# A fused attention and convolution step on one core: queries and keys of a head asked for nine blocks ahead, two V buffers, weights asked for twelve steps earlier

## The chip, the cores and the metric

The kernel runs on one core of a Trainium2 chip. The metric is the device time of one execution in microseconds (us); the program before was run three times. Traces and profile come from one execution taken by the hardware profiler.

## What is computed

One layer of a streaming encoder over 1024 prompt frames and 32 sample frames (the 32 next frames of a stream with 512 cached ones), width 1024. Cut to what matters here:

```python
h = rmsnorm(x, norm_g)                       # 1056 frames x 1024
q, k, v, f, ga, ua, ub, gb, ma, mb = split(h @ w_in)
q, k = rmsnorm(q) * 64 ** -0.5, rmsnorm(k)   # 16 heads of 64
c = cumsum(log_sigmoid(f + b_f))             # one forget sum per head
p = softmax(causal(q @ k.T + c_q - c_k))     # per head
ya = (p @ v * silu(ga)) @ w_pa
u = ua * sigmoid(ub)                         # causal depthwise conv, 31 taps
yb = (silu(layernorm(conv(u))) * silu(gb)) @ w_pb
y = x + (sigmoid(ma) * ya + sigmoid(mb) * yb) @ w_out
```

Outputs are y, the keys, values, forget logs and the last 30 convolution rows.

## The kernel before, in words

Channels lie on partitions, the 1056 frames on the free axis. Each projection is done for 128 output channels at a time (`steps`): three chunks of 352 frames, each summed over eight slices of 128 input channels, each slice as three float16 matmuls (high weights by high input, low by high, high by low, L183). One slice is one **step**: three matmuls, then `beat()`, which runs what the planner has put at this step.

**Weights** come in batches of two blocks (`Batch`). A batch is loaded as two `raw` tiles (L109, four buffers), its power is measured (ACT `junk` L117, POOL `topb` L120, PE `tot` L126, DVE `sc` L157), and it is split into `wh` (ACT L138) and `wl` (DVE L141). `begin()` runs when the first block of a batch is projected, and sets the next batch's work at fixed steps from there: measured at 3 and 13, split at 29 and 39, its last `wl` pieces at 34 and 44; and it asks for the raw weights of the batch after that at steps 17 and 27. A batch is 48 steps.

**Stages**, in order: the token rows are turned and the first convolution block projected (`x_split`, in three column chunks, with a table of jobs by step); the values; the convolution inputs with the keys and queries between them, which go to scratch in DRAM (`s_k`, `s_q`, each a high and a low part); the gate `ga`; attention, beside which the gates `gb`, `ma` and `mb` are projected; then three output projections.

**Attention.** `seq` holds 16 heads of eight blocks (`Block`, 128 queries each); four `Sample` blocks for the cached stream are put in after the first block of heads 3, 7, 11 and 15. Loop step n works on `seq[n]`: `start(seq[n + 3])` makes the scores of the block three further on (`QB` by `KB` L1094, `QA` by `KA` L1095); then mask and maximum (DVE L1097, L1099), exponent (ACT L1102), scaling (POOL L1105); `turn()` transposes the probabilities of `seq[n]` (PE `ptr` L1119, copied by ACT or DVE L1122); `fill(4)` does four steps of a gate projection, whose chunk is read out by ACT into one of three `t` tiles (L930, L932) and stored by a DMA (L933). That projection has one PSUM bank (`pq`). Two loop steps after the last block of a head, `values()` multiplies by V (PE `po`, forty matmuls, L1138), ACT and DVE put the result into `ot` (L1142, L1143; in odd heads L1145 multiplies by the gate `ga`, loaded at L1127), and in odd heads a DMA stores it (L1147).

A head's queries and keys are eight DMAs on SP's queue (`Head.load`, L948 to L955: six of 256 KB, two of 16 KB), into two sets of buffers in turn. They are asked for when `seq[n + 5]` is the head's first block, that is in block 3 of the head before; the head's first scores are made in block 5 of it. V is one DMA (L962) into a single buffer, asked for after the values of the head before.

**Orders.** In attention the orders of PE and SP are those of the code; SP takes its DMAs strictly one after another, and one that waits (for data, for a buffer, or for the DMA eight before it to have landed) holds up those behind it. The other engines' orders there come from the scheduler's own simulated time. In the stages before, PE, DVE and ACT stand in the order of the code and SP's is the scheduler's.

Of the kernel before, what the change touches and what calls it, by code (L numbers as in the profile page):

```python
# [8 lines left out]
F32 = mybir.dt.float32  # L9
# [13 lines left out]
H = 16  # L23
# [30 lines left out]
def build(tc, xT, xt, wv, wf, ckT, cv, clT, stT, vec, cst, yT, kT, vO, lfO, cpT, csT):  # L54
# [4 lines left out]
    def pool(name, bufs=1, stack=es, **kw):  # L59
        return stack.enter_context(tc.tile_pool(name=name, bufs=bufs, reuse_waits="tile", **kw))  # L60
# [29 lines left out]
    class Batch:  # L90
# [31 lines left out]
        def total(self):  # L122
            pool, tag = totals[-1]
            self.ps = pool.tile([128, 512], F32, name="tot", tag=tag)
            if self.n == 2:
                nc.tensor.matmul(self.ps[:, :2], ones_b, self.topb, start=True, stop=True)  # L126
            else:
                for i in range(2):
                    nc.tensor.matmul(self.ps[:, 0:1], ones_b, self.topb[:, i:i + 1], start=(i == 0), stop=(i == 1))
# [7 lines left out]
        def high(self, i, wh, raw, ks):  # L137
            nc.scalar.mul(wh[:, ks, :], raw[:, ks, :], self.s[:, i:i + 1])  # L138

        def low(self, i, wl, wh, raw, ks):  # L140
            nc.vector.scalar_tensor_tensor(wl[:, ks, :], raw[:, ks, :], self.s[:, i:i + 1], wh[:, ks, :],  # L141
                                           op0=ALU.mult, op1=ALU.subtract)
# [78 lines left out]
    def begin():  # L221

        if not plan:
            return
        b = plan.pop(0)
        after = plan[0] if plan else None
        t = pace["tick"]
        jobs = [(25, b.total), (27, b.power)]
        if b.n == 2:
            jobs += [(3, lambda: b.stage(0)), (13, lambda: b.stage(1))]  # L230
            for i, n in ((0, 29), (1, 39)):
                jobs.append((n, lambda i=i: b.split(i)))
                jobs += [(n + 1 + 2 * p, lambda i=i, p=p: b.rest(i, p)) for p in range(3)]
        else:
            jobs += [(3 + 10 * i, lambda i=i: b.stage(i)) for i in range(2)]
            jobs.append((29, lambda: split.__setitem__(b.keys[0], split_v(b.keys[0][1], b))))
        if after:
            jobs += [(17 + 10 * i, after.load) for i in range(after.n)]
        prep.extend((t + n, fn) for n, fn in sorted(jobs, key=lambda e: e[0]))

    def steps(key, rh, rl, pspool, evac):
# [38 lines left out]
    class Banks:  # L280

        n = 0
# [230 lines left out]
    def squares(t, act=True, sl=slice(0, D), acc=None):  # L513
        r = rows(t)
        acc = rs9[:r, t:t + 1] if acc is None else acc
        sq = xip.tile([128, D], F32, name="sq", tag="sq", bufs=2)[:r, sl]
        x = xtok[t][:r, sl]
        if act:
            nc.scalar.activation(sq, x, AF.Square, accum_out=acc)
        else:  # L520
            nc.vector.scalar_tensor_tensor(sq, x, 1.0, x, op0=ALU.mult, op1=ALU.mult, accum_out=acc)

    def root(t0, nt):

        rs = rs9[:, t0:t0 + nt]
        v, y = [xip.tile([128, 4], F32, name=f"n4{i}", tag=f"n4{i}", bufs=2)[:, :nt] for i in range(2)]
        nc.vector.tensor_scalar(v, rs, 1.0 / D, EPS, op0=ALU.mult, op1=ALU.add)
        nc.scalar.activation(y, v, AF.Ln)
        nc.scalar.activation(y, y, AF.Exp, scale=-0.5)
        return lambda: newton(rs, v, y)  # L530

    def scale(t, h, pool=False):
        r = rows(t)
        x, f = xtok[t][:r, half[h]], rs9[:r, t:t + 1]
        if pool:
            nc.gpsimd.tensor_scalar(x, x, f, 1.0, op0=ALU.mult, op1=ALU.mult)
        else:
            nc.vector.tensor_scalar(x, x, f, None, op0=ALU.mult)
# [60 lines left out]
    def known(i):  # L599
        recs[i].power(psq[:, i + 1:i + 2], 1)  # L600
# [23 lines left out]
    def rooted(t0, nt):  # L624
        steps_of[t0] = root(t0, nt)
# [12 lines left out]
    for f in range(8):  # L638
# [14 lines left out]
    x_split(0, ws0, u0, {  # L653
        0: [lambda: top(1), lambda: squares(2, False)],
        1: [lambda: squares(3)],
        2: [lambda: total(2), lambda: high(0, 1), lambda: low(0, 1)],
        3: [lambda: known(1), lambda: squares(4, False), lambda: high(1, 0), lambda: low(1, 0)],
        4: [lambda: rooted(2, 3), lambda: high(0, 2)],
        5: [lambda: steps_of[2](), lambda: scale(2, 0), lambda: scale(3, 0, True), lambda: scale(4, 0), lambda: low(0, 2)],
        6: [lambda: scale(3, 1, True), lambda: scale(2, 1), lambda: high(1, 1), lambda: low(1, 1)],  # L660
        7: [lambda: scale(4, 1), lambda: high(1, 2), lambda: low(1, 2)]})
# [38 lines left out]
    def split_v(c, rec):  # L700
        wh2, wl2, raws2 = [], [], rec.raws
        for raw in raws2:
            with tc.high_priority(offset=1500):
                wh, wl = [vp.tile([128, 4, VC], F16, name=a, tag=a, bufs=4) for a in ("vwh", "vwl")]
                rec.high(0, wh, raw, slice(0, 4))
                for k in (0, 2):
                    rec.low(0, wl, wh, raw, slice(k, k + 2))
            wh2.append(wh)
            wl2.append(wl)

        def running():
            ps = pj.tile([128, 512], F32, name="pjs", tag="pj")
            for n in range(2):
                for j in range(4):
                    nc.tensor.matmul(ps[32 * j:32 * j + 32, :VC], xsm[:, 2 * j + n, :],
                                     raws2[j // 2][:, (2 * j + n) % 4, :], start=(n == 0), stop=(n == 1))
            pace["credit"] -= 1.3
            later(4, lambda: gathered(ps))

        def gathered(ps):  # L720
            v4 = vp.tile([TS, 4, VC], F32, name="v4", tag="v4", bufs=1)
            for j in range(4):
                nc.scalar.copy(v4[:, j, :], ps[32 * j:32 * j + 32, :VC])
            vs = vp.tile([TS, VC], F32, name="vs", tag="vs", bufs=1)
            nc.vector.tensor_reduce(vs, v4.rearrange("p j n -> p n j"), axis=AX.X, op=ALU.add)
            nc.vector.tensor_copy(z[:TS, 8, 4 * c:4 * c + 4], vs[:, 256:])
            nc.sync.dma_start(vO[T:, 256 * c:256 * c + 256], vs[:, :256])
            nc.sync.dma_start(s_vs[:, 256 * c:256 * c + 256], vs[:, :256])

        later(14, running)  # L730
        return wh2, wl2, rec.inv
# [4 lines left out]
    for c in range(4):  # L736
# [13 lines left out]
        pace["rate"] = R_V  # L750
        wh2, wl2, inv = split.pop(("v", c))
        begin()
        for t in range(8):
            ps = pj.tile([128, 512], F32, name="pjv", tag="pj")
            n = 0
# [181 lines left out]
    class Head:  # L937
# [20 lines left out]

        def load_v(self):
            h = self.h  # L960
            self.V = hp.tile([128, 8, 64], F32, name="V", tag="V", bufs=1)
            nc.sync.dma_start(self.V, s_v[:, :, 64 * h:64 * h + 64].rearrange("b t d -> t b d"))  # L962

    pace["rate"] = R_U
# [3 lines left out]
    hp = pool("hp", 2, stack=p2, side="right")  # L968
    heads = [Head(h) for h in range(H)]
# [31 lines left out]
    def fill(n):  # L1001
        for _ in range(n):
            next(flow, None)
# [145 lines left out]
    seq = []  # L1149
# [5 lines left out]
    def start(b):  # L1155
        if getattr(b, "i", 1) == 0:
            h = b.head
            if h.h % 2 == 0:
                h.ot = heads[h.h + 1].ot = ap.tile([128, T], F32, name="ot", tag="ot", bufs=2)
        b.scores()  # L1160

    def pending(b):
        return isinstance(b, Sample) or b.i % 2
# [36 lines left out]
    ln = layernorm()  # L1200
    sides["shift"] = ap.tile([128, TT], F32, name="shift", bufs=1)
    nc.sync.dma_start(sides["shift"], s_m)
    start(seq[0])
    fill(8)
    start(seq[1])
# [2 lines left out]
    for n, b in enumerate(seq):  # L1208
        if n + 3 < len(seq):
            start(seq[n + 3])  # L1210
        if n + 5 < len(seq) and getattr(seq[n + 5], "i", 1) == 0:
            seq[n + 5].head.load()
        if n + 6 < len(seq) and isinstance(seq[n + 6], Sample):
            seq[n + 6].load()
        if isinstance(b, Sample):
            fill(4)
            b.turn()
        else:
            b.turn()
            fill(4 if b.i > 2 or b.head.h != 8 else 0)  # L1220
        if n >= 2 and pending(seq[n - 2]):
            seq[n - 2].values()
        if n >= 3 and isinstance(seq[n - 3], Sample):
            seq[n - 3].finish()
        if n >= 2 and getattr(seq[n - 2], "i", 0) == 7 and seq[n - 2].head.h + 1 < H:
            heads[seq[n - 2].head.h + 1].load_v()
        if "ready" in sides:
            next(ln, None)
    for b in seq[-2:]:
# [16 lines left out]
    class Banks3:  # L1246
        n = 0
# [383 lines left out]
```

## Time and profile before

| what | us |
|---|---|
| median of three runs | 1451.53 |
| lowest and highest run | 1445.54, 1453.81 |
| the profiled execution | 1445.9 |
| its span in the trace | 1443.9 |
| stage: start, to the first values | 0 to 60 |
| stage: values and convolution inputs | 60 to 215 |
| stage: keys, queries, convolution inputs, gate ga | 215 to 577 |
| stage: attention with gates | 577 to about 1155 |
| stage: output projections | 1155 to 1444 |

How to read it: a row of the windows view gives for each engine the busy time in that stretch and the number of instructions, then the clock that TensorE was granted (1.00 is full), the share of time that the DMA engines were busy, and the rate. A row of the waits view names who waited, for whom, the total in us, how often, and the longest. A row of the timeline gives start, length, engine, line, operation, tiles, and in brackets the idle time just before it with what ended it. A row of the chain gives start, length and the piece of work on the chain that ended last.

### The profile page before, as it was taken

What the parts mean: (1) busy time and instruction counts of PE and PEld (TensorE: products, weight loads), DVE (VectorE), ACT (ScalarE), POOL (GpSimd) and SP (SyncE); (2) the same over time, 40 slices, a digit from 0 to 9 for tenths busy, and PEclk for the clock granted to TensorE, in tenths of its full rate; (3) what the DMA queues carried; (4) which work ended last, traced back from release to release, by engine and by line L of the source; (5) the groups of instructions that cost most, each with busy time, mean ns of one, the idle gap of its engine ahead of it and who ended that gap; (6) DMA issues with size and microseconds to landing.
All of it is one profiled execution on the core that took longest, in us unless ns stands there. A gap on an engine that the chain in (4) does not pass through costs nothing.

```text
span 1443.9 us, 24762 instructions
## 1 busy us (share of the span) xinstructions
PE 1347.8 (93%) x9383; PEld 1020.0 (71%) x9383; DVE 976.5 (68%) x1534; ACT 723.0 (50%) x1360; POOL 496.5 (34%) x548
## 2 busy tenths in 40 slices
PE   8999999999999999787989788978888999999999
PEld 5687866666666666565666566656665689999999
DVE  6787888869798988656767645544444459455664
ACT  6544547575768535444544454534543465423321
POOL 2000126265748302333333322211211228545653
PEclk9999999999999999999999999999999999999999
DMA  6242434373435232335343543453444197743462
GB/s 233 92 148 85 125 89 130 109 195 116 131 121 168 100 128 95 99 102 148 108 130 107 155 116 83 121 149 88 116 116 124 49 359 258 233 135 120 144 202 73
DMA packets 113495, 194.96 MB, mean 135 GB/s; under 512 B 34080, under 2 KB 80032, under 8 KB 113376
## 3 DMA queue, kind: packets, MB, share of 16 engines
q1 hardware_dynamic: 113232, 193.31, 43.9%
q8 instruction: 74, 1.21, 0.4%
q14 instruction: 45, 0.37, 0.1%
q10 hardware_dynamic: 144, 0.07, 0.0%
HBM read 127.68 MB, written 65.64 MB: 134 GB/s over the span
## 4 chain that ended last, share of the span: by engine, by line
PE 71%; DMA 10%; DVE 5%; SPq 5%; ACT 4%; issue 3%; POOL 1%; ACTq 0%; DVEq 0%; POOLq 0%
PE pj L183 47%; PE pjv L760 6%; PE pj L1463 5%; PE po L1138 5%; DMA KA<-s_ak 5%; PE ptr L1119 3%; DMA raw<-wf 2%; DMA KA<-s_k 2%; PE psS L1095 1%; DVE y L368 1%; PE psS L1094 1%; ACT t L932 1%; DVE nm L1099 1%; DVE wl L141 1%; ACT P L1102 1%
## 5 line engine op out<-in xcount | busy, mean ns | idle before, releaser
L183 PE MATMUL pj<-xh,wh 128*128 128x352 f16 (+2 forms) x1536 | 489.0, 318 | 8.2 <-ACT t L932 6.9
L183 PE MATMUL pj<-xh,wl 128*128 128x352 f16 (+2 forms) x1536 | 488.1, 318 | 0.7 <-DVE wl L141 0.6
L183 PE MATMUL pj<-xl,wh 128*128 128x352 f16 (+2 forms) x1536 | 487.5, 317 | 0.1
L183 PEld LDWEIGHTS <-wh 128*128 128x128 f16 x3072 | 305.4, 99 | 165.4 <-issue 2.6
L368 DVE SCALAR_TENSOR_TENSOR y<-u,vec_t,y 128x1086 f32<-128x1086 f32 x240 | 342.6, 1428 | 9.5 <-ACT y L365 6.6
L1105 POOL TENSOR_SCALAR P<-P,nm 128x128 f32<-128x128 f32 (+7 forms) x128 | 119.1, 931 | 336.7 <-DVE nm L1104 281.7
L183 PEld LDWEIGHTS <-wl 128*128 128x128 f16 x1536 | 152.6, 99 | 84.4 <-issue 10.7
L141 DVE SCALAR_TENSOR_TENSOR wl<-raw,sc,wh 128x384 f16<-128x384 f32 (+1 forms) x192 | 119.1, 655 | 30.5 <-ACT wh L138 30.5
L1122 ACT COPY pt<-ptr 128x512 f32<-128x512 f32 (+3 forms) x128 | 64.4, 503 | 143.9 <-PE ptr L1119 143.3
L1102 ACT ACTIVATE P<-psS,nm 128x128 f32<-128x128 f32 (+7 forms) x128 | 94.8, 741 | 65.5 <-DVE nm L1099 52.0
L1094 PE MATMUL psS<-KB,QB 128*128 128x256 f32 (+2 forms) x192 | 82.7, 432 | 39.7 <-DMA KB<-s_k 33.8
L1097 DVE TENSOR_TENSOR psS<-psS,cmask 128x128 f32<-128x128 f32 x128 | 37.7, 295 | 118.2 <-PE psS L1095 117.7
L1099 DVE TENSOR_REDUCE nm<-psS 128x1 f32<-128x128 f32 (+7 forms) x128 | 96.3, 754 | 8.5 <-DVE psS L1097 0.5
L1095 PE MATMUL psS<-KA,QA 68*128 68x256 f32 (+2 forms) x192 | 70.1, 366 | 30.1 <-DMA KA<-s_ak 24.6
L1119 PE MATMUL ptr<-ident,P 128*128 128x128 f32 x576 | 93.6, 294 | 1.2 <-ACT pt L1122 1.2
L175 POOL TENSOR_TENSOR wl<-raw,wh 128x384 fp32r<-128x384 f32 (+1 forms) x51 | 63.4, 1271 | 74.6 <-ACT wh L172 58.7
L1119 PEld LDWEIGHTS ptr<-ident,P 128*128 128x128 f32 x576 | 77.2, 153 | 6.9 <-ACT pt L1122 1.5
L1094 PEld LDWEIGHTS psS<-KB,QB 128*128 128x128 f32 x192 | 37.5, 195 | 57.3 <-issue 39.9
L138 ACT ACTIVATE wh<-raw,sc 128x1024 f16<-128x1024 f32 (+1 forms) x68 | 72.7, 1089 | 7.8 <-DVE sc L158 7.5
L869 POOL TENSOR_TENSOR sql<-sqf,sqh 128x352 fp32r<-128x352 f32 x48 | 58.7, 1224 | 50.7 <-ACT sqh L866 50.6
L1138 PE MATMUL po<-pt,V 128*64 128x256 f32 x640 | 72.8, 382 | 0.3 <-ACT pts L1051 0.3
L117 ACT ACTIVATE junk<-raw 128x1024 bf16<-128x1024 f32 x62 | 65.2, 1052 | 12.9 <-DMA raw<-wf 12.8
(271 smaller groups left out, 2574.8 us busy)
## 6 DMA issues: line engine op xcount, KB each, us to landing
raw<-wf SPq DMA_DIRECT2D x92, 512.0 KB
QB<-s_q SPq DMA_DIRECT2D x32, 256.0 KB
KB<-s_k SPq DMA_DIRECT2D x32, 256.0 KB
kT<-qn SPq DMA_DIRECT2D x8, 528.0 KB
s_ga<-t SPq DMA_DIRECT2D x24, 176.0 KB
s_gb<-t SPq DMA_DIRECT2D x24, 176.0 KB
s_ma<-t SPq DMA_DIRECT2D x24, 176.0 KB
s_mb<-t SPq DMA_DIRECT2D x24, 176.0 KB
```

The source lines that it names most:

```text
L138: nc.scalar.mul(wh[:, ks, :], raw[:, ks, :], self.s[:, i:i + 1])
L141: nc.vector.scalar_tensor_tensor(wl[:, ks, :], raw[:, ks, :], self.s[:, i:i + 1], wh[:, ks, :], op0=ALU.mult, op1=ALU.subtract)
L183: nc.tensor.matmul(ps, a[:, kt, :], b(kt, sl), start=(first and n == 0), stop=(last and n == N - 1))
L368: t = nc.vector.scalar_tensor_tensor(y, u[:, i:i + CW], w, y, op0=ALU.mult, op1=ALU.add)
L760: nc.tensor.matmul(ps[:, :VC], a, b, start=(n == 0), stop=(n == 23))
L1094: nc.tensor.matmul(ps[:, b, :wm], QB[:, qsl], KB[:, ksl], start=True, stop=False)
L1095: nc.tensor.matmul(ps[:, b, :wm], QA[:, qsl], KA[:, ksl], start=False, stop=True)
L1099: nc.vector.tensor_reduce(nm[:, 0:1], ps[:, :nb, :w], axis=AX.XY, op=ALU.max, negate=True)
L1102: nc.scalar.activation(P[:, :nk].rearrange("p (b w) -> p b w", b=nb), ps[:, :nb, :w], AF.Exp, bias=nm[:, 0:1], accum_out=nm[:, 1:2])
L1105: nc.gpsimd.tensor_scalar(P[:, :nk], P[:, :nk], nm[:, 2:3], 1.0, op0=ALU.mult, op1=ALU.mult)
L1119: nc.tensor.transpose(pt[:, 128 * j:128 * j + 128], P[:, 128 * (4 * u + j):128 * (4 * u + j) + 128], ident)
L1138: nc.tensor.matmul(po[rows], V[:, j, :], parts[c][:, j, :], start=(c % 2 == 0 and j < 2), stop=(c % 2 == 1 and j >= 2 * c))
```

## The change

Five edits: `after.load` stands at steps 5 and 15 instead of 17 and 27; in the first chunk of `x_split` the power of the second weight block (`total(2)`, `known(1)`, `high(1, 0)`, `low(1, 0)`) comes one step later; V has two buffers; a head's queries and keys are asked for nine blocks ahead, those of head 1 before the loop; the next head's V is asked for in block 3.

```diff
@@ Batch planning, begin() @@
-            jobs += [(17 + 10 * i, after.load) for i in range(after.n)]
+            jobs += [(5 + 10 * i, after.load) for i in range(after.n)]
@@ x_split(0, ...) @@
-        2: [lambda: total(2), lambda: high(0, 1), lambda: low(0, 1)],
-        3: [lambda: known(1), lambda: squares(4, False), lambda: high(1, 0), lambda: low(1, 0)],
-        4: [lambda: rooted(2, 3), lambda: high(0, 2)],
+        2: [lambda: high(0, 1), lambda: low(0, 1)],
+        3: [lambda: total(2), lambda: squares(4, False)],
+        4: [lambda: known(1), lambda: rooted(2, 3), lambda: high(1, 0), lambda: low(1, 0), lambda: high(0, 2)],
@@ Head.load_v @@
-            self.V = hp.tile([128, 8, 64], F32, name="V", tag="V", bufs=1)
+            self.V = hp.tile([128, 8, 64], F32, name="V", tag="V", bufs=2)
@@ before the attention loop @@
     nc.sync.dma_start(sides["shift"], s_m)
+    heads[1].load()
     start(seq[0])
@@ the attention loop @@
-        if n + 5 < len(seq) and getattr(seq[n + 5], "i", 1) == 0:
-            seq[n + 5].head.load()
+        if n + 9 < len(seq) and getattr(seq[n + 9], "i", 1) == 0:
+            seq[n + 9].head.load()
         if n + 6 < len(seq) and isinstance(seq[n + 6], Sample):
             seq[n + 6].load()
+        if getattr(b, "i", 0) == 3 and b.head.h + 1 < H:
+            heads[b.head.h + 1].load_v()
...
-        if n >= 2 and getattr(seq[n - 2], "i", 0) == 7 and seq[n - 2].head.h + 1 < H:
-            heads[seq[n - 2].head.h + 1].load_v()
```

First place: SP's queue in attention around head 4, before the change. `s_gb<-t` is a gate store, `s_o<-ot` the attention output of heads 2 and 3, V the values of head 4, and the eight rows after it head 5's queries and keys.

```order
L1127 DMA ga<-s_ga 128x1024
L933 DMA s_gb<-t 128x352
L1147 DMA s_o<-ot 128x1024
L962 DMA V<-s_v 128x8x64
L948 DMA QB<-s_q 64x1024
L949 DMA QB<-s_q 64x1024
L950 DMA KB<-s_k 64x1024
L951 DMA KB<-s_k 64x1024
L952 DMA QA<-s_q 64x1024
L953 DMA QA<-s_aq 4x1024
L954 DMA KA<-s_k 64x1024
L955 DMA KA<-s_ak 4x1024
```

The same place after the change. V is now head 5's, asked for in block 3 of head 4, and the queries and keys at the end, of which the first rows are shown, are head 6's, asked for in block 7 of head 4.

```order
L1127 DMA ga<-s_ga 128x1024
L109 DMA raw<-wf 128x1024
L933 DMA s_gb<-t 128x352
L1147 DMA s_o<-ot 128x1024
L962 DMA V<-s_v 128x8x64
L109 DMA raw<-wf 128x1024
L933 DMA s_gb<-t 128x352 x2
L948 DMA QB<-s_q 64x1024
L949 DMA QB<-s_q 64x1024
L950 DMA KB<-s_k 64x1024
L951 DMA KB<-s_k 64x1024
```

The eight loads no longer stand right behind the output store and the V load: they come six blocks ahead of the head's first scores instead of two, and V is asked for six blocks ahead of its use.

Second place: SP's queue in the stage of keys and queries, where the scheduler had put head 0's load among the stores of a query block (`s_q<-qh`, `s_q<-ql`). Rows with a minus leave this place.

```order
-L109 DMA raw<-wf 128x1024
-L896 DMA s_q<-ql 128x352
-L109 DMA raw<-wf 128x1024
-L948 DMA QB<-s_q 64x1024
-L949 DMA QB<-s_q 64x1024
-L950 DMA KB<-s_k 64x1024
-L951 DMA KB<-s_k 64x1024
-L895 DMA s_q<-qh 128x352
-L952 DMA QA<-s_q 64x1024
-L896 DMA s_q<-ql 128x352
```

After the change the load stands behind the last query block's stores, ahead of two raw weight loads.

```order
L328 DMA s_y<-y 128x1024
L329 DMA s_y<-y 128x32
L948 DMA QB<-s_q 64x1024
L949 DMA QB<-s_q 64x1024
L950 DMA KB<-s_k 64x1024
L951 DMA KB<-s_k 64x1024
L952 DMA QA<-s_q 64x1024
L953 DMA QA<-s_aq 4x1024
L954 DMA KA<-s_k 64x1024
L955 DMA KA<-s_ak 4x1024
L962 DMA V<-s_v 128x8x64
L109 DMA raw<-wf 128x1024 x2
```

Outside attention the raw loads of the weights keep their places among SP's other rows.

Third place: PE at the start. `ptx` are transposes of the token rows, `pj<-tops` is `total(2)`, the matmuls of L183 are the first projections.

```order
 L573 MATMUL ptx<-ident,xtok 128x128 x6
-L477 MATMUL pj<-tops_147,ones_w 128x1
 L183 LDWEIGHTS wh_216
...
 L183 MATMUL pj<-xl,wh_216 128x256
 L573 MATMUL ptx<-ident,xtok 128x128 x2
+L477 MATMUL pj<-tops_147,ones_w 128x1
 L183 LDWEIGHTS wh_216
```

Three matmuls and two transposes now go ahead of `total(2)`. It is the only move on PE in the whole program.

## The prediction

> **What bounds the kernel now.** I read the page first, for who is busy and what the chain that ended last runs through.
>
> ```profile
> PE 1347.8 (93%) x9383; PEld 1020.0 (71%) x9383; DVE 976.5 (68%) x1534; ACT 723.0 (50%) x1360; POOL 496.5 (34%) x548
> PE 71%; DMA 10%; DVE 5%; SPq 5%; ACT 4%; issue 3%; POOL 1%; ACTq 0%; DVEq 0%; POOLq 0%
> PE pj L183 47%; PE pjv L760 6%; PE pj L1463 5%; PE po L1138 5%; DMA KA<-s_ak 5%; PE ptr L1119 3%; DMA raw<-wf 2%; DMA KA<-s_k 2%; PE psS L1095 1%; DVE y L368 1%; PE psS L1094 1%; ACT t L932 1%; DVE nm L1099 1%; DVE wl L141 1%; ACT P L1102 1%
> ```
>
> TensorE is the bound, but a tenth of the chain lies in DMA, and most of that in the loads of a head's keys (`KA`). The windows view by stage says where PE is not full.
>
> ```profile
> 215.00:577.00 362.00, 356.54 (x2386) 235.03 (x2385) 304.47 (x369) 227.14 (x400) 177.15 (x170) 1.00 0.40 129
> 600.00:1155.00 555.00, 480.84 (x3340) 341.42 (x3340) 306.05 (x663) 261.88 (x560) 133.35 (x210) 0.93 0.42 113
> 1185.00:1356.00 171.00, 171.00 (x1077) 171.00 (x1077) 106.68 (x115) 71.33 (x93) 97.64 (x69) 1.00 0.57 187
> ```
>
> The first busy figure is PE's. In the key and query stage and in the output projections it has almost no idle time at full clock. In attention it idles 74 of 555 us, and the granted clock is 0.93, the only long stage where it is under 1. DVE (306) and ACT (262) are far from full, and the DMA engines stand at 0.42. So I asked for PE's waits from 585 to 1160 us.
>
> ```profile
> PE psS L1094 <- DMA KB<-s_k: 33.8, 10, 5.2
> PE psS L1095 <- DMA KA<-s_ak: 24.6, 11, 2.9
> PE pj L183 <- ACT t L932: 6.4, 9, 2.0
> PE psS L1095 <- DMA KA<-s_k: 5.4, 3, 1.9
> PE psS L1094 <- issue: 2.4, 1, 2.4
> ```
>
> The scores of a head's first block wait for its keys: 33.8 + 24.6 + 5.4, and 2.4 that the trace puts to "issue" at the same place of head 14, make **66.2 us**. Why the keys are late is on SP's queue, here for head 5:
>
> ```profile
> 736.42 0.32 SPq L1147 DMA_DIRECT2D s_o<-ot  x1
> 736.84 0.55 SPq L962 DMA_DIRECT2D V<-s_v  x1
> 737.43 0.88 SPq L948 DMA_DIRECT2D QB<-s_q  x1
> 741.95 0.48 SPq L955 DMA_DIRECT2D KA<-s_ak  x1
> 745.73 0.36 PE L1094 MATMUL psS<-KB,QB 128*128 128x256 f32 x1 [2.38 <-DMA KB<-s_k]
> 748.67 0.55 PE L1095 MATMUL psS<-KA,QA 68*128 68x256 f32 x1 [2.58 <-DMA KA<-s_ak]
> ```
>
> The eight loads go out at 737.4 to 742.4, behind a store and a V load that themselves wait for the head before, and the last has landed when PE goes on at 748.7: 11.3 us after the first was issued. PE was there two and a half microseconds before `KB`, and waits again for `KA`.
>
> **Part 1: keys nine blocks ahead.** The new place is six blocks before the first scores. The undisturbed pace of a head is in the windows from one `po` to the next:
>
> ```profile
> 729.53:765.13 35.60, 30.48 (x199) 21.72 (x201) 23.82 (x46) 17.86 (x37) 9.46 (x13) 0.90 0.44 118
> 765.13:794.01 28.88, 27.74 (x199) 20.19 (x200) 21.66 (x37) 13.34 (x31) 10.12 (x13) 1.00 0.47 125
> 780.15 0.36 PE L1095 MATMUL psS<-KA,QA 68*128 68x256 f32 x1 [1.07 <-DMA KA<-s_ak]
> ```
>
> The second held a wait of only 1.07 us and took 28.88 us for the same 199 matmuls; 28.88 / 8 is 3.6 us a block, so six blocks are 21.7 us of lead against 11.3 needed. The buffers asked for are those of the head two back, whose last scores were made three blocks before. So I cost the wait at nothing and the gain at 66.2 us; what covers it is 10 us of spare lead. With a lead shorter by more than that, each microsecond would come back at fifteen heads.
>
> A second gain hangs on the first. The chain's pieces after a long wait and after the short one:
>
> ```profile
> 604.55 3.07 PE pj L183 x12
> 749.22 1.28 PE ptr L1119 x6
> 750.50 3.49 PE pj L183 x12
> 780.51 0.66 PE ptr L1119 x6
> 781.17 1.79 PE pj L183 x12
> 1107.23 2.62 PE pj L183 x12
> ```
>
> The same twelve matmuls take 3.49 us after a wait of five and 1.79 after one of one: PE comes out of a wait at about half speed. There are thirteen slow ones between 604.55 and 1107.23 (3.07 the first, 2.62 the last); added up they exceed thirteen times 1.79 by 17 us, and the six transposes ahead of them cost up to 0.62 us more each time, 8 us. So **25 us** of slow clock goes with the waits, 91 us together.
>
> The Trainium skill (TensorE: Matmul & The Clock Gate, section What's actually happening) has PE's clock halved after an idle window of about 3.4 us and whole again after as long a busy one. The trace agrees in the factor, 3.49 against 1.79. By the page each cold spell would cost half of 3.4 us, an estimate of 1.7, and thirteen 22 us where the rows give 25.
>
> As a bound, windows from the second head to the fifteenth:
>
> ```profile
> 619.66:657.13 37.47, 30.98 (x200) 22.16 (x201) 23.00 (x47) 18.48 (x37) 10.45 (x14) 0.91 0.45 126
> 1084.16:1122.07 37.91, 30.86 (x213) 21.47 (x215) 15.05 (x36) 13.54 (x32) 6.80 (x13) 0.91 0.48 119
> ```
>
> Fourteen windows lie from 619.66 to 1122.07, 502.4 us; fourteen undisturbed ones are 404.3. The difference, 98, also holds the sample blocks and the layer norm's matmuls, so 91 is not too small.
>
> **What is late next.** At 28.9 instead of 35.6 us a head, DVE has as much to do in less time: 23 to 24 us in an early head, some 81% where the undisturbed one had 75%, and PE waits for `t` more often (6.4 us over nine cases now). I take 1 us more in each of the first eight heads, which still carry convolution taps, **8 us** in all; the bounds are 0 (the undisturbed head, 1.1 us idle) and 2.4 us a head, were DVE to lose the full difference of 23.8 and 21.4, some 19 us.
>
> **Part 2: V in two buffers.**
>
> ```profile
> SPq L1147 <- DVE ot L1145: 42.4, 6, 8.5
> SPq L962 <- PE po L1138: 36.8, 8, 6.2
> ```
>
> SP stood 36.8 us at V until `po` had freed it, with the keys behind it. That wait goes, and its worth is already in the 66.2. V has six blocks to land. The store's 42.4 stays, but the keys come later in the queue, behind V. Nothing added.
>
> **Part 3: raw weights at steps 5 and 15.** In SP's order this shows in attention only. The buffer asked for was last read at steps 34 and 44 of the batch before, 19 steps, or almost five blocks, 17 us earlier; a raw row that had to wait would hold stores and keys behind it. No such wait stands in attention now, and the loads are not waited for by PE: 0, bounds 0 and the 19 us of DVE lag above.
>
> **Part 4: head 0's load.**
>
> ```profile
> 300.00:310.00 10.00, 8.37 (x56) 5.47 (x55) 7.34 (x6) 7.11 (x15) 6.92 (x7) 1.00 0.57 158
> 320.00:330.00 10.00, 9.03 (x61) 5.86 (x59) 7.71 (x7) 9.53 (x19) 7.85 (x8) 1.00 0.95 300
> 330.00:340.00 10.00, 8.65 (x58) 5.57 (x57) 9.89 (x10) 5.66 (x13) 8.27 (x7) 1.00 0.30 105
> 484.64 4.78 SPq L109 DMA_DIRECT2D raw<-wf  x2
> 556.60 18.16 SPq L933 DMA_DIRECT2D s_ga<-t  x6
> ```
>
> PE lost 4.0 us in these 30, around the place that the load leaves; I take half, 2 us gained (0 to 4). At its new place it delays two raw loads, now at 484.64, by the some 5 us that eight issues took above, and head 1's load delays gate stores at 556.6 likewise; three `t` tiles and five banks cover them, each good for a chunk of 24 matmuls, 3.6 us at 1.79 for twelve. I take 1 us lost (0 to 5).
>
> **Part 5: the start.**
>
> ```profile
> PE pj L477 <- ACT junk L596: 1.8, 1, 1.8
> PE pj L183 <- DVE wl L141: 0.6, 1, 0.6
> PE pj L183 <- ACT wh L138: 0.5, 1, 0.5
> 15.30 1.22 DVE L521 SCALAR_TENSOR_TENSOR sq<-xtok 128x1024 f32<-128x1024 f32 x1
> ```
>
> `total(2)` waits 1.8 us now; with work ahead of it that goes. But the power of the second weight then stands behind this 1.22 us square sum on DVE, and the two waits at its split, 1.1 us, grow by up to as much. I take 0, between 1.8 gained and 1.2 lost.
>
> **The sum**: 66.2 + 25 − 8 + 2 − 1 = 84 us. The profiled execution took 1445.9 (span 1443.9), so 1362 for its like; it lies 5.6 under the median of the runs shown, 1451.53, at the low end of their spread. Waits that end with a DMA should be what spreads them, so I add only 2: **1364 us**.
>
> **The rivals.**
>
> *DVE takes over.* The head would go at DVE's pace: 19 us of new waits for 8, and ACT's exponents behind it as much again, some 25 in all. For it: DVE over 80% in early heads. Against: 1.1 us idle at 28.88. Gives 1364 + 17, **1381**.
>
> *The keys are still late.* They go out in front of `ga`, a weight load and stores; if those and the eight shared the way so that landing took 24 us instead of 11, against 21.7 of lead, 2.4 us would stay at each of fifteen heads: 1364 + 36, **1400**. Against: a DMA share of 0.42.
>
> The Trainium skill (DMA: Bandwidth & Descriptors, section Queues, rings and completion order) says that each DMA engine takes a queue's descriptors in ring order, which speaks against asking early: what is asked later stands behind 1.5 MB of keys. No row here separates that from SP's own order.
>
> *Slower: the gate store behind the keys.* The store after the eight loads needs a free place among eight outstanding DMAs. Chunks follow each other at two blocks, 7.2 us; three `t` tiles let a store be about 21 us late. Beyond that ACT cannot read out the one bank `pq`, PE stops, and SP's lag feeds on itself. From 6 us beyond it in each of fifteen heads (90 us) the change loses; at 8 us it gives 1364 + 120, **1484**. Against: the store follows the loads directly before too, and waits for `t` are 6.4 us in all.
>
> *It doesn't do what it says*: the early load waits on SP for the buffers of the head two back and goes out where it did: **1446**. Against: those scores are three blocks old.
>
> **Chances.** The forecast, 1350 to 1376: 0.63. DVE: 0.17. Late keys: 0.08. Under 1350, when the slow clock was worth more: 0.04. Not as it says: 0.04. Slower: 0.04. The range from 1347 to 1398 takes in the forecast, DVE and the lower edge of late keys. A measurement tells about 0.5% here: faster 0.92, same 0.04, slower 0.04.
>
> **What would show it.** The waits for `KB` and `KA` should fall from 66 us to under 5, the clock in attention go from 0.93 to 0.99, a head take 28 to 30 us, and DVE's share there rise to about two thirds. The stages before 577 and after attention should keep their lengths to 3 us. It is wrong if PE waits as long for `t`, P or transposes as it did for the keys, or if SP shows rows of L109 or L933 waiting in front of L948.

## The result, and the profile after

| | before | after |
|---|---|---|
| median, us (lowest to highest; four runs each, side by side on one chip) | 1449.98 (1445.54 to 1453.81) | 1370.53 (1368.33 to 1374.55) |
| profiled execution | 1445.9 | 1370.8 |
| its span, mean granted clock | 1443.9, 0.969 | 1368.9, 0.993 |

The ratio is 0.9456, 95% interval 0.942 to 0.9493: faster by 5.4%. The profiled executions differ by 75.1 us; the sum had said 84.

The same three rows of the page, after the change:

```profile
PE 1321.6 (97%) x9383; PEld 1004.6 (73%) x9383; DVE 976.6 (71%) x1534; ACT 721.7 (53%) x1360; POOL 500.2 (37%) x548
PE 73%; DVE 8%; DMA 6%; ACT 6%; issue 4%; SPq 1%; POOL 1%; ACTq 0%; DVEq 0%; POOLq 0%
PE pj L183 51%; PE pjv L760 6%; PE pj L1464 5%; DMA raw<-wf 4%; PE po L1138 3%; PE ptr L1119 2%; DVE y L368 2%; DVE nm L1099 2%; ACT P L1102 2%; PE psS L1094 1%; PE psS L1095 1%; DVE wl L141 1%; ACT t L932 1%; ACT junk L117 1%; DMA a<-s_o 1%
```

The keys have left the chain. But DMA still holds 6% of it, now in the raw weights (`raw<-wf`, 4%). The windows by stage, with the edges moved with the program:

```profile
215.00:575.00 360.00, 355.05 (x2377) 234.16 (x2375) 306.25 (x367) 226.95 (x400) 179.92 (x171) 1.00 0.43 135
600.00:1076.00 476.00, 448.10 (x3308) 322.37 (x3307) 303.88 (x663) 258.19 (x558) 133.69 (x207) 0.99 0.48 130
1106.00:1281.00 175.00, 174.55 (x1097) 174.55 (x1098) 110.52 (x119) 72.64 (x95) 97.74 (x69) 1.00 0.58 191
```

In attention PE now idles 28 of 476 us where it idled 74 of 555, and its clock is 0.99. One head in its middle, from `po` to `po`:

```profile
739.00:768.28 29.28, 27.71 (x198) 20.14 (x197) 21.94 (x39) 14.52 (x33) 10.10 (x13) 1.00 0.43 106
```

PE's waits between 570 and 1095 us, where the kernel before (570 to 1160) had 66.2 us at the keys and some 12 elsewhere:

```profile
PE pj L183 <- ACT t L932: 17.1, 19, 2.4
PE psS L1094 <- ACT P L1102: 8.9, 6, 2.6
PE psn L1168 <- DVE ot L1143: 1.6, 1, 1.6
PE psS L1027 <- ACT P L1102: 1.2, 1, 1.2
PE tot L126 <- DVE ot L1143: 0.3, 1, 0.3
```

No row for `KB` or `KA` is left. What is left is 29.1 us, and 27.2 of it ends with ACT. So the next question is what ACT waits for (570 to 1110 us):

```profile
ACT P L1102 <- DVE nm L1099: 64.1, 60, 2.8
ACT pt L1122 <- PE ptr L1119: 59.0, 55, 3.9
ACT junk L117 <- DMA raw<-wf: 37.7, 16, 4.7
```

The first two are ACT waiting for the work that it is there to do. The third is not: ACT stands 37.7 us at `junk`, the measuring of raw weights, because they have not landed; before, this row had 12.8 us in 11 cases. One case, in the timeline:

```profile
903.54 0.58 SPq L109 DMA_DIRECT2D raw<-wf  x1
908.50 0.31 PE L183 MATMUL pj<-xl,wh 128*128 128x352 f16 x1
911.59 1.06 ACT L117 ACTIVATE junk<-raw 128x1024 bf16<-128x1024 f32 x1 [3.81 <-DMA raw<-wf]
912.65 0.53 ACT L932 ACTIVATE t<-pj,sc 128x352 f32<-128x352 f32 x1
913.23 0.45 PE L183 MATMUL pj<-xh,wh 128*128 128x352 f16 x1 [2.43 <-ACT t L932]
```

The gate chunk is complete when the matmul of 908.50 ends, and ACT is free. But `junk` is ahead of the read-out `t` on ACT's queue, and its weights were asked for at 903.54. They land 8 us later; only then come `junk`, `t`, and the next chunk on PE, which needs the bank. In the code `junk` stands 46 steps, over eleven blocks, behind that load (load at step 5 or 15, `junk` at step 3 or 13 of the next batch). On ACT the order is that of the scheduler's simulated time, which puts it so early that it runs 3.7 us (the first case, 571.1 to 574.8) to 8 us (this one) after the load was asked for, in all twenty cases.

Where the 75 us came from is read at the fixed marks of the chain, the long run of the output projections, before and then after:

```profile
1181.55 172.15 PE pj L183 x1081
```

```profile
1106.45 172.24 PE pj L183 x1081
```

It starts 75.1 us earlier and has the same length. The first scores of attention came at 573.5 us before and at 575.7 now, so attention gained 77.3 and the stages ahead of it lost 2.2. Between these marks PE does the same 3649 matmuls; their busy time fell from 528.5 to 500.3 us and PE's idle time from 79.6 to 30.4, so of the 77.3 us 28 are matmuls that ran faster and 49 are waits.

### The profile page after: what moved, and what is told of

Same layout as the page of the kernel before. It is cut to its first block, busy times and chain, and to the rows that moved or that the text cites. A ratio compares the mean times of both kernels' runs of the same rounds, so it can differ in the third digit from the quotient of the medians.

```text
span 1368.9 us, 24793 instructions
## 1 busy us (share of the span) xinstructions
PE 1321.6 (97%) x9383; PEld 1004.6 (73%) x9383; DVE 976.6 (71%) x1534; ACT 721.7 (53%) x1360; POOL 500.2 (37%) x548
## 4 chain that ended last, share of the span: by engine, by line
PE 73%; DVE 8%; DMA 6%; ACT 6%; issue 4%; SPq 1%; POOL 1%; ACTq 0%; DVEq 0%; POOLq 0%
PE pj L183 51%; PE pjv L760 6%; PE pj L1464 5%; DMA raw<-wf 4%; PE po L1138 3%; PE ptr L1119 2%; DVE y L368 2%; DVE nm L1099 2%; ACT P L1102 2%; PE psS L1094 1%; PE psS L1095 1%; DVE wl L141 1%; ACT t L932 1%; ACT junk L117 1%; DMA a<-s_o 1%
## 5 line engine op out<-in xcount | busy, mean ns | idle before, releaser
L183 PE MATMUL pj<-xh,wh 128*128 128x352 f16 (+2 forms) x1536 | 483.8, 315 | 20.9 <-ACT t L932 17.1
L183 PE MATMUL pj<-xh,wl 128*128 128x352 f16 (+2 forms) x1536 | 483.3, 315 | 0.4 <-DVE wl L141 0.4
L183 PE MATMUL pj<-xl,wh 128*128 128x352 f16 (+2 forms) x1536 | 483.2, 315 | 0.4 <-DVE xl L576 0.2
L183 PEld LDWEIGHTS <-wh 128*128 128x128 f16 x3072 | 302.2, 98 | 164.0 <-ACT wh L138 3.6
L1105 POOL TENSOR_SCALAR P<-P,nm 128x128 f32<-128x128 f32 (+7 forms) x128 | 122.1, 955 | 281.0 <-DVE nm L1104 231.2
L183 PEld LDWEIGHTS <-wl 128*128 128x128 f16 x1536 | 151.1, 98 | 93.7 <-issue 22.4
L117 ACT ACTIVATE junk<-raw 128x1024 bf16<-128x1024 f32 x62 | 65.2, 1052 | 37.8 <-DMA raw<-wf 37.7
L1119 PE MATMUL ptr<-ident,P 128*128 128x128 f32 x576 | 85.0, 274 | 0.0
L1119 PEld LDWEIGHTS ptr<-ident,P 128*128 128x128 f32 x576 | 69.8, 142 | 5.7 <-ACT pt L1122 0.2
L120 POOL CAST topb<-tops 128x2 bf16<-128x2 f32 x35 | 12.9, 367 | 162.8 <-ACT junk L117 112.8
L894 POOL TENSOR_TENSOR ql<-qn,qh 128x352 fp32r<-128x352 f32 (+1 forms) x48 | 62.8, 1311 | 22.2 <-ACT qh L893 22.2
```

The lines of the kernel that those rows point to most:

```text
L117: nc.scalar.activation(junk[:, :raw.shape[1] * raw.shape[2]], raw.rearrange("p a b -> p (a b)"), AF.Square, accum_out=self.tops[:, i:i + 1])
L183: nc.tensor.matmul(ps, a[:, kt, :], b(kt, sl), start=(first and n == 0), stop=(last and n == N - 1))
L1105: nc.gpsimd.tensor_scalar(P[:, :nk], P[:, :nk], nm[:, 2:3], 1.0, op0=ALU.mult, op1=ALU.mult)
L1119: nc.tensor.transpose(pt[:, 128 * j:128 * j + 128], P[:, 128 * (4 * u + j):128 * (4 * u + j) + 128], ident)
```

## The experiments

Four theories. **Lead**: the keys were late because they were asked for two blocks before their use, with 11.3 us needed. **V**: SP stood at V with the keys behind it, and freeing V is what helps. **Clock**: beside the waits PE lost some 25 us in slow matmuls after them. **ACT**: the new waits are ACT standing at raw weights that have not landed; its rival there was that the raw edit (steps 5 and 15) does the harm. Each kernel was timed beside the kernel before on the same chip, but not all on one chip; ratios are to the kernel before there, with 95% intervals.

**Keys alone.** The lead of nine and head 1's load ahead of the loop; V, the raw steps and the start as before.

```diff
+    heads[1].load()
...
-        if n + 5 < len(seq) and getattr(seq[n + 5], "i", 1) == 0:
-            seq[n + 5].head.load()
+        if n + 9 < len(seq) and getattr(seq[n + 9], "i", 1) == 0:
+            seq[n + 9].head.load()
```

> Only the queries and keys nine blocks ahead (head 1's before the loop); V, the raw weights and the start as before. The lead theory (the eight loads need 11 us from the first issue to the last landing, two blocks of 3.6 us are too short, six are enough): nearly the whole gain, 1366 to 1376 us, no waits of the scores for KB or KA, though SP still stands some 37 us at V. The V theory (the single V buffer holds the keys back on SP, and the lead matters little): no more than a third of the gain, 1415 or above.

Measured 1377.53, ratio 0.9505 (0.9476 to 0.9534), 1.5 us outside the lead theory's band. No wait for keys is left, although SP still stands at V:

```profile
SPq L962 <- PE po L1138: 32.0, 8, 6.2
```

So the lead is the cause; for V, raw steps and start together 7 us are left between the medians.

**V alone.** Two V buffers, V asked for in block 3; the rest as before.

```diff
-            self.V = hp.tile([128, 8, 64], F32, name="V", tag="V", bufs=1)
+            self.V = hp.tile([128, 8, 64], F32, name="V", tag="V", bufs=2)
...
+        if getattr(b, "i", 0) == 3 and b.head.h + 1 < H:
+            heads[b.head.h + 1].load_v()
...
-        if n >= 2 and getattr(seq[n - 2], "i", 0) == 7 and seq[n - 2].head.h + 1 < H:
-            heads[seq[n - 2].head.h + 1].load_v()
```

> Only V: two buffers, asked for in block 3 of the head before; keys still five ahead. The V theory: most of the gain, 1370 to 1400 us, waits for KB and KA under 20 us. The lead theory: SP's 36.8 us at V go, so the keys go out earlier by up to that in all, but two blocks still do not cover 11 us: waits for KB and KA fall from 64 to some 35 to 60 us, time 1410 to 1445 us.

Measured 1439.46, ratio 0.9943 (0.9925 to 0.9961), inside the lead theory's band. The keys are still late:

```profile
PE psS L1095 <- DMA KA<-s_ak: 26.0, 10, 3.1
PE psS L1094 <- DMA KB<-s_k: 21.8, 9, 3.5
PE psS L1095 <- DMA KA<-s_k: 5.0, 3, 2.2
```

52.8 us of 63.8 stay. With V out of the way they go out earlier by too little. The V theory falls.

**A lead of seven, a lead of six.** The changed kernel with `n + 9` made `n + 7` or `n + 6`, and no load ahead of the loop.

```diff
-    heads[1].load()
...
-        if n + 9 < len(seq) and getattr(seq[n + 9], "i", 1) == 0:
-            seq[n + 9].head.load()
+        if n + 7 < len(seq) and getattr(seq[n + 7], "i", 1) == 0:
+            seq[n + 7].head.load()
```

> The changed kernel with keys asked for seven blocks ahead instead of nine (four blocks before the first scores, 14.4 us at 3.6 us a block). The lead theory: as good as nine, 1366 to 1376 us, since 11.3 us are needed; waits for KB and KA under 10 us. If the landing takes longer than in the trace of before because of what else is in the queue (the rival of late keys): 1385 to 1410 us with 20 us or more of such waits.

> The changed kernel with keys asked for six blocks ahead (three blocks before the first scores, 10.8 us). The lead theory: just short, since 11.3 us are needed and SP may be held at the output store ahead of them: 1 to 3 us of wait at a head, 10 to 40 us of waits for KB and KA in all, time 1380 to 1420 us. The V theory: still 1370, since V is out of the way.

Six: 1415.85, ratio 0.9766 (0.9736 to 0.9797), with 23.5 us of waits for keys, inside the band. Seven: 1387.36, ratio 0.9583 (0.9554 to 0.9612), 11 us over its band, and not for the keys:

```profile
PE pj L183 <- ACT t L932: 25.4, 20, 4.4
PE psS L1094 <- ACT P L1102: 12.7, 7, 3.0
PE psS L1027 <- ACT P L1102: 1.5, 2, 1.2
PE po L1138 <- ACT pts L1051: 0.9, 1, 0.9
PE psS L1095 <- DMA KA<-s_k: 0.4, 1, 0.4
```

The keys cost 0.4 us. The waits that end with ACT are 40.5 us against 27.2 with nine ahead, and this was the first sign that ACT, not DVE, makes the new ones. ACT itself stands 38.5 us at `junk` here, hardly more than with nine (37.7); why that costs PE more with seven was not traced.

**The raw steps back at 17 and 27**, the rest of the changed kernel kept.

```diff
-            jobs += [(5 + 10 * i, after.load) for i in range(after.n)]
+            jobs += [(17 + 10 * i, after.load) for i in range(after.n)]
```

> The changed kernel with the raw weights asked for at steps 17 and 27 again. The prediction's step (part 3 is worth nothing): the same as the changed kernel within 5 us, 1366 to 1376. The rival (asked early, the measuring of the weights on ACT is put behind a transfer that has not landed; it waits 37.7 us for raw in the changed kernel and 12.8 before, and the gate read-out behind it makes PE wait 17.1 instead of 6.4): faster by some 10 us, 1358 to 1363, with ACT's waits for raw back at 13 and PE's for t at 7.

Measured 1378.87, ratio 0.9508 (0.948 to 0.9536), 3 us over the band of the prediction's step; ACT still stands at raw weights:

```profile
ACT junk L117 <- DMA raw<-wf: 34.8, 16, 5.9
```

Asking late does not help: the rival falls. Asking early probably gains some 7 us: keys alone, which differs from this kernel in V and the start, has the same ratio (0.9505), and the changed kernel with the old start, timed on the same chip (0.9428 to 0.9475, below), is faster with an interval that just misses this one. It is not settled, since this interval and the changed kernel's just overlap.

**The old start**, the rest of the changed kernel kept.

```diff
-        2: [lambda: high(0, 1), lambda: low(0, 1)],
-        3: [lambda: total(2), lambda: squares(4, False)],
...
+        2: [lambda: total(2), lambda: high(0, 1), lambda: low(0, 1)],
+        3: [lambda: known(1), lambda: squares(4, False), lambda: high(1, 0), lambda: low(1, 0)],
```

> The changed kernel with the table of jobs of the first chunk as before. The prediction's step (part 5 is worth nothing, between 1.8 gained and 1.2 lost): the same within 2 us, and the first values still start at 73 to 76 us. The rival (the 3 us by which the changed kernel's trace was later at its first values, 76.0 against 73.0, come from the start): 3 us faster, first values at 73.

Measured 1368.28, ratio 0.9452 (0.9428 to 0.9475): no difference in time from the changed kernel that can be told. The first values start at 73.2, as the rival has it; one trace of each does not settle whether the edit moved them (see below).

**Measuring behind the last read-out.** The changed kernel, with `junk` in attention issued behind the latest `t` in the code's order, so that it cannot stand ahead of the read-outs of a whole batch. The line that this adds moves the line numbers behind it by one.

```diff
+            with (tc.issue_after(sides["t"].ins) if "t" in sides else ExitStack()):
+                nc.scalar.activation(junk[:, :raw.shape[1] * raw.shape[2]], raw.rearrange("p a b -> p (a b)"),
+                                     AF.Square, accum_out=self.tops[:, i:i + 1])
...
-                nc.scalar.mul(t, ps, inv)
+                sides["t"] = nc.scalar.mul(t, ps, inv)
```

> The changed kernel, in attention ACT measures a raw weight only behind the last gate read-out that the code has put ahead of it, some 46 steps after the load was asked for, instead of where the scheduler's simulated time puts it. If ACT's 37.7 us of waits for raw weights are what makes PE wait longer for t and P: those waits fall under 5 us, PE's waits for t from 17.1 to 5 to 9, and the time to 1355 to 1363 us. If PE waits for t because ACT is simply fuller at 28.5 us a head: PE's waits for t stay at 14 us or more and the time at 1368 to 1374.

Measured 1352.11, ratio 0.9339 (0.9319 to 0.9359): 18 us faster than the changed kernel (17 by the ratios), 3 more than expected at best. PE's waits:

```profile
PE psS L1095 <- ACT P L1103: 5.9, 4, 2.6
PE pj L184 <- ACT t L933: 5.0, 13, 1.2
PE psS L1028 <- ACT P L1103: 1.5, 2, 1.2
```

The waits for `t` fall from 17.1 to 5.0, under the 6.4 of the kernel before, with DVE's work the same. ACT's row for `junk` is gone from its list, and the order of its other work is the same but for a few neighbours. The ACT theory holds for the waits for `t`. Those for `P` fall only from 10.1 to 7.4 us (before the change they were some 2); what makes the rest was not tested, and DVE, for which ACT waits there, is not ruled out.

**Warm matmuls.** The kernel before, with 24 matmuls ahead of the first scores of heads 1 to 15; their results, in the scores' bank, are written over unread, and nothing is left out.

```diff
+            if i == 0 and self.head.h:
+                for k in range(24):
+                    nc.tensor.matmul(ps[:, 0, :CH], xh[:, 0, :128], xh[:, 0, :CH], start=True, stop=True)
```

> The kernel before with added work: 24 matmuls that nobody reads (128x352 in float16, 3.6 us in all) on PE ahead of the first scores of each head but the first, written to the scores' own bank and overwritten; keys asked for as before. If 25 us of the loss are slow clock that the idle wait brings about (the prediction's second gain): PE sits busy through two thirds of each wait, the keys come no sooner, the clock in attention rises from 0.93 to 0.97 or more, and the time falls by 25 less some 8 lost at the three heads with short waits: 1425 to 1440 us, faster with 54 us of added work. If slow matmuls behind a wait come from something else (data still landing, the queue starting up): 1449 plus 8 or more, 1455 to 1500.

Measured 1435.75, ratio 0.99 (0.9873 to 0.9928). The attention window, 600 to 1155 us as shown of the kernel before:

```profile
600.00:1155.00 555.00, 521.40 (x3760) 369.57 (x3759) 310.97 (x672) 265.72 (x567) 140.71 (x214) 0.98 0.44 119
```

Its waits for keys (the edit moves the lines of the scores by three):

```profile
PE psS L1098 <- DMA KA<-s_ak: 14.7, 8, 2.6
PE psS L1098 <- DMA KA<-s_k: 8.4, 4, 2.9
...
PE psS L1097 <- DMA KB<-s_k: 1.8, 3, 0.7
```

One group of 24 has its first start at 665.1 and its last at 668.6 in the trace; at 1.79 us for twelve it takes 3.6 us, so fifteen are 54 us of added work. They fill 38.9 us of the waits (63.8 fell to 24.9) and so should cost 15; the kernel is 14 faster (1%, with an interval clear of 1), at a clock of 0.98 for 0.93. That puts the slow clock at 29 us, an estimate made apart from any change in the loads.

**Measuring late in three other kernels**: the same edit on the kernel before, on keys alone, and on leads of seven and six.

> The kernel before, with ACT's measuring of raw weights in attention only behind the last gate read-out, nothing else. If the measuring became costly only when the keys stopped covering it: the waits for keys stay and hide it, 1440 to 1450 us. If it cost its 18 us before as well: 1430 us.

> Only the keys nine blocks ahead, plus the late measuring; V, raw weights and start as before. If what V in two buffers and raw weights at 5 and 15 are worth (the changed kernel against keys alone, 7 us) comes only through where ACT meets unlanded weights: the same as the changed kernel with late measuring, 1350 to 1356 us. If V's wait on SP costs by itself: 1357 to 1362.

> The changed kernel with keys seven blocks ahead and the late measuring. Seven blocks left 0.4 us of waits for keys, yet took 17 us more than nine. If that is ACT held at weights whose load now meets the keys' load in the queue: late measuring gives the same with seven as with nine, 1350 to 1357 us. If the lead itself is too short somewhere: 1362 to 1372.

> The changed kernel with keys six blocks ahead (three before the first scores, 10.8 us at 3.6 us a block) and the late measuring. With ACT out of the way what is left is the lead: the 23.5 us of waits for KB and KA that six blocks left, and the slow clock behind some of them, stay: 1368 to 1385 us, against 1347 with seven and 1352 with nine. If those waits came from the queue's weights being late on ACT too: 1345 to 1357.

The medians; the kernels ran on several chips, so the ratios, each to the kernel before on its own chip, are what compares.

| kernel | as it was | with late measuring | ratio of the latter |
|---|---|---|---|
| before | 1449.60 | 1442.15 | 0.9949 (0.9931 to 0.9968) |
| keys alone | 1377.53 | 1356.49 | 0.9357 (0.9333 to 0.9382) |
| changed (nine) | 1370.53 | 1352.11 | 0.9339 (0.9319 to 0.9359) |
| seven | 1387.36 | 1347.10 | 0.9299 (0.9274 to 0.9323) |
| six | 1415.85 | 1392.41 | 0.9626 (0.9597 to 0.9654) |

Before the change the same fault cost 7 us, after it 18. ACT's own waits at `junk` had grown in step, from 12.8 to 37.7 us; that the waits for keys covered part of it, as the expectation has it, is possible and not shown. On seven late measuring gives 40 us, 3 more than expected at best, and seven then has the **lowest time of all**, though its interval still touches that of nine:

```profile
600.00:1050.00 450.00, 437.77 (x3267) 316.83 (x3267) 300.89 (x656) 257.60 (x558) 136.38 (x208) 1.00 0.51 136
```

PE idles 12 of 450 us there. So seven blocks of lead are enough, and what the first run of seven lost was ACT. Keys alone with late measuring, at 1356.49 between the bands of its two theories, is 4 us behind the changed kernel with it (under 3 by the ratios), and the intervals overlap: V, raw steps and start are worth 0 to 7 us, no more closely known.

Six is still slow, 7 us over its band, and here the keys are the cause. Its waits, and SP's queue and PE at one of seven heads with late keys, all of them heads whose load stands behind an output store:

```profile
PE psS L1096 <- DMA KA<-s_ak: 15.3, 6, 3.0
PE psS L1095 <- ACT P L1103: 9.5, 8, 2.6
PE psS L1095 <- DMA KB<-s_k: 5.7, 2, 3.0
...
PE psS L1096 <- DMA KA<-s_k: 2.0, 1, 2.0
```

```profile
722.13 0.32 SPq L1148 DMA_DIRECT2D s_o<-ot  x1
722.54 1.18 SPq L949 DMA_DIRECT2D QB<-s_q  x1
727.34 0.48 SPq L956 DMA_DIRECT2D KA<-s_ak  x1
733.16 0.55 PE L1096 MATMUL psS<-KA,QA 68*128 68x256 f32 x1 [2.30 <-DMA KA<-s_ak]
```

The loads go out as soon as the store lets SP go, and the last is there 10.6 us after the first was issued. Six ahead leaves three blocks, 10.8 us at 3.6, minus what SP stands at the store. That part decides: at the seven late heads PE stood ready 5.6 to 8.0 us after the first issue, while at the eight other heads, whose load has no such store ahead of it, the first issue came 10.2 to 16.6 us before the first scores and no wait for keys is left. The head after the one above is such a case:

```profile
750.13 0.45 SPq L949 DMA_DIRECT2D QB<-s_q  x1
762.14 0.41 PE L1095 MATMUL psS<-KB,QB 128*128 128x256 f32 x1
```

With seven ahead the loads stand in front of the store instead of behind it and go out 15 us or more before the scores, but for head 1 (10.2 us, no wait).

## Why the prediction was right, and which term was not

*Keys, 66.2 us.* Right. The waits are gone, and with the lead alone too. The 11.3 us that the prediction read as needed fits the traces: loads that came out 8.0 us ahead or less were late, those that came out 10.2 us ahead or more were not. Its spare lead of 10 us was real: two blocks of it could be given back.

*Slow clock, 25 us.* Right, a little small. Attention gained 77.3 us with 66.2 of key waits gone and 17 of other waits added (29.1 after, some 12 before); the 28 that remain are the 28 by which PE's busy time fell, and agree with the 29 of the warm matmuls. (The prediction's thirteen slow pieces add up to 16 us by the rows of the chain, not 17.)

*New waits, 8 us, put to DVE.* **This step failed**, in size and, for the greater part, in cause. "What is late next" argued from DVE's share, 75 to 81% of a head, and took each wait for `t` as a sign of it. They came to 17 us, near the end of its bounds (19), and the experiment that moves `junk` on ACT's queue took 15 us of waits and 18 us of time away with DVE's work unchanged. That the size stayed inside bounds drawn for another engine is luck. The view that would have told it is ACT's own waits: the kernel before already showed 12.8 us at `junk`.

*Raw steps, 0.* The runs point to some 7 us gained, under 3 with late measuring, neither of them settled; no loss shows. The reason given, that "the loads are not waited for by PE", missed the chain of which ACT is the middle: PE waits for `t`, `t` stands behind `junk`, and `junk` waits for the load.

*V, nothing of its own.* V is asked for about 50 us ahead of its use (781.15 to 832.87 for head 7), fourteen blocks and not the six that the texts above give it. The term is right as a part of the whole: alone it gives 8 us, with 11 us of key waits gone (63.8 to 52.8); with the lead, SP's 32.0 us at V cost nothing that was told apart from 7 us.

*Head 0's load, 2 gained and 1 lost.* The stage of keys and queries regained 0.8 us at the old place, and no PE wait stands at the new ones. Too small to test.

*The start, 0.* As a trade it is right: `total(2)` waits 0.3 where it waited 1.8, and the split behind it 2.4 where it waited 0.5. But the first values begin at 76.1 us instead of 73.2 (not at 60, as the table of stages has it). How much of that is the edit's doing is open: the seven kernels with the new start have them between 73.4 and 76.3, 75.4 in the mean, the seven with the old one between 73.2 and 75.9, 74.2 in the mean, one trace each. 1.3 us of it is PE's wait at `tot` for POOL's `topb` (0.7 before, 2.0 after), which is 2.0 in keys alone too, with the old start.

*The sum.* 66.2 + 28 − 17 + 0.8 − 3 = 75, against 84: nine more lost to new waits and three at the start, three given back by the clock. Of the rivals, "DVE takes over" came near in size (25 us of new waits for 17) and had the wrong engine; late keys, the gate store behind the keys, and no effect did not occur.

*A rule of the Trainium skill* (TensorE: Matmul & The Clock Gate, section What's actually happening) was quoted with an idle window of about 3.4 us ahead of a slow clock. The twelve-matmul pieces of the chain after the change say that less can be enough:

```profile
608.53 1.79 PE pj L183 x12
...
783.27 3.46 PE pj L183 x12
...
913.23 3.61 PE pj L183 x12
```

The piece at 913.23 follows the single wait of 2.43 us shown above, with transposes up to it, and takes twice the usual 1.79; the one at 783.27 follows a wait of 2.23. But the piece at 608.53 comes 1.5 us after a wait of 2.46, and is at full speed:

```profile
607.04 0.45 PE L1094 MATMUL psS<-KB,QB 128*128 128x384 f32 x1 [2.46 <-ACT P L1102]
```

The measurement decides: waits of 2.2 to 2.4 us halved the clock at two places here, and one as long did not, so the length of the wait alone does not tell. What else does was not found.

*Left open*: whether seven is better than nine with late measuring. It is 5 us faster with intervals that touch, and 2.9 of these lie ahead of attention, in the start that varies.

## What to carry to other kernels

Set the lead of a load by its own time from first issue to last landing, and count what its queue may stand at ahead of it: 14.4 us were enough here, and 10.8 were not where the load stood behind a store. When a large wait on the bound engine goes, look up the waits of the engines that feed it (ACT's row at `junk`), not only their shares, since a small wait there can grow once the large one is gone (12.8 to 37.7 us here). Where a scheduler orders an engine by simulated time, look for instructions that it has put close behind a load, and tie them to something later.

## What the runs showed that was not expected

54 us of unread matmuls made the kernel before 14 us faster (0.99, 0.9873 to 0.9928): they filled 38.9 us of its waits, and the clock in attention went from 0.93 to 0.98.

A lead of seven was 17 us slower than nine with 0.4 us of waits for keys, and at least as fast as nine once `junk` was tied: the comparison of two leads was decided by another engine's queue.

With late measuring, six was 45 us slower than seven with only 23 us of waits for keys, at seven heads: the mean clock is 0.984 against 0.996, which of a span of some 1389 us is an estimate of 17 us more, and 2.8 us of the rest lie at the start.
